# Encoder layer: places of the first W_up tiles in the sample's output projection, and the number of leading steps in the prompt's

## The chip, the cores and the metric

The kernel runs on one core of one Trainium2 chip. The metric is the device time of one execution in microseconds (us). Of several executions the median counts. Five engines work side by side, each on its own queue in order: TensorE (PE, matrix products; its weight loads are PEld), VectorE (DVE), ScalarE (ACT), GpSimd (POOL) and SyncE (SP), which here starts most of the DMA transfers. The order in each queue is fixed when the program is built; at run time an engine waits at the head of its queue until what the instruction needs is there.

## The reference

One layer of a bidirectional encoder, applied with the same weights to two request groups: `sample` (512 tokens) and `prompt` (1024 tokens), with a model width of 1024 and a hidden width of 4096. What matters here is the second half of the layer:

```python
    mixed = jax.nn.sigmoid(gate_na) * y_na + jax.nn.sigmoid(gate_fn) * y_fn
    x = x + mixed @ w_out
    a = jax.nn.relu(rmsnorm(x, g_mlp) @ w_up)
    return x + (a * a) @ w_down
```

`w_out` is 1024 x 1024, `w_up` 1024 x 4096. All is in fp32. The kernel makes an fp32 product from three products of two parts each: a number is split into a rounded part `hi` and the rest `lo`, and hi\*hi, hi\*lo and lo\*hi are added up in PSUM (`mm3`, line 122).

## The kernel before, in words

**Order of the whole.** The sample is done first (attention, Fourier mixing, gates, output projection, W_up), then the prompt, and at the end W_down for both. The program is written in one order, and a scheduler that fixes each engine's queue when the program is built takes from it, by its own model of times, what it holds to be ready, earlier lines first. So products of different tiles can stand mixed on PE. `behind(marks)` keeps instructions after given ones, and `pinned()` after the last ones written so far.

**A weight tile** (`weights`, line 142) is fetched by DMA to one of two raw places `w_raw` (512 KB), its `hi` is made by ACT (line 152) and its `lo` by POOL (line 153; one W_out tile has it on DVE). Only when POOL is done is the raw place free for the next fetch.

**The sample's output projection** (`Layer.project_out`, line 1079). W_out is cut into eight tiles, numbers 0 to 3 for the left half of the output columns, 4 to 7 for the right. Their places (line 460): number 0 in the pool `mlp` (tag `w`, two places), 1 to 4 in the pool `out` (tag `wo`, four places), 5 in two Fourier tiles, 6 in the shared `w_hi`/`w_lo` places, 7 in the second `w` place. First come the left halves of the four token tiles t = 0 to 3 (128 tokens each), then their right halves. After each right half the tile is added to x (DVE, line 1105), stored, and normed: ACT squares and sums (line 174), DVE does nine short steps on one column (lines 175 to 183) and a wide one (line 184). The normed tile is then transposed on PE (line 194) and split by ACT and DVE (lines 133 and 134) into `h2T`, the input of W_up.

**W_up of the sample** (`Up`, line 1123). 32 tiles f of 128 hidden columns; `load(f)` fetches and splits one, into the shared `w_hi`/`w_lo` places for f % 4 of 0 or 1, else into the two `w` places. `load(0)` is called after the third right half, 1 and 2 after the fourth, the others when `up(f)` begins, though the scheduler moves them ahead as soon as places are free. Tiles 0, 1 and 2 are multiplied in two halves of 256 tokens: their first halves need only token tiles 0 and 1, and the transposes of tiles 2 and 3 stand between them. The other tiles take 512 tokens at once. `run` then walks over pairs of tiles; beside each pair it does a step of `combine` (sums of W_down blocks on POOL) and a step of `reading` (norm and transposes of the prompt's first tiles).

**The prompt's output projection** (`Halves.project_out`, line 1274). Eight token tiles with a left and a right half each: 16 steps n = 0 to 15 of 24 matmuls. The list `steps` gives their order: the first four left halves, then right and left in turn, then the last four right halves (n = 12 to 15). The banks for even n are of the tag `mm`, for odd n of `o`. The k-th right half (k = 0 to 7) is normed as above. For odd k four differences of the tiles k and k-1 are formed on DVE (line 1342). An even k makes two turns, an odd k five: a turn (`turn`, line 1263) is four transposes into a PSUM bank (four banks, tags `t` and `s`) and two splits on ACT and DVE. `due` says after which step's product the turns stand: two steps after the right half (one after for n = 14, so k = 5 and k = 6 both have theirs after the last product, and k = 7 after the first products of W_up). Turns into `t2` and `t3` need the places of W_out's left half and wait until the step `freed`, one after the last left half. `ahead` splits the first W_up pair on ACT and POOL beside it. W_out's right half (tiles 4 to 7) goes to the places `w` and `r` of the pool `mlp`. After the last product come the turns of k = 5 and 6, the first W_up products with `b11` and `b21` (lines 1358 and 1361), the turns of k = 7 and the W_up product with `t2`.

Of the kernel before, what the change touches and what calls it, by code (L numbers as in the profile page):

```python
# [68 lines left out]
class Layer:  # L69
# [279 lines left out]
    def run(self, order):  # L349
# [4 lines left out]
        hp, close_hT = self.open("hT_0", "left")  # L354
        hT, folded = self.new_hT(hp, order[0][1], NM)
        for i, (name, T) in enumerate(order):
# [5 lines left out]
            if i == 0:  # L362
                with pool("first", "right") as p:
# [8 lines left out]
                    marks = self.mark((mybir.EngineType.SP,))  # L372
                    w0 = self.qk_weights(0)

                    rest = self.tables(marks)
# [20 lines left out]
            if small:  # L396
                ap, hp_, mp = (right.enter_context(pool(f"{n}_{name}", "right")) for n in ("acc", "hid", "mlp"))
# [8 lines left out]
            else:  # L406
                fn = None
                p = right_fn.enter_context(pool(f"na_{name}", "right"))
# [34 lines left out]
            with pool(f"u_{name}", "right") as up:  # L443
# [5 lines left out]
                with pool(f"dft_{name}", "right") as p:  # L449
                    fT, marks = self.fourier_positions(p, fp, name, T, u, cos, sin if small else sin + [  # L450
                        self.sines(p.tile([128, 5 * 522], F32R, name="sin"), name, T, 1)])
# [6 lines left out]
            if small:  # L458
                po = out.enter_context(pool(f"out_{name}", "right"))
# [3 lines left out]
            else:  # L463
                hp_ = right.enter_context(pool(f"hid_{name}", "right"))
# [3 lines left out]
            h2T = self.merge_fn(br, hp_ if small else br, T, fT, mixed, sig, gate, wout, marks)  # L468
            close_br()
            close_fT()  # L470
            if not small:
                mp = right.enter_context(pool(f"mlp_{name}", "right"))
                places += [(mp, [128, 2, 512], "w", 2)] * 2 + [(mp, [128, 2, 512], "r", 2)] * 2
                with self.behind(self.mark()):
                    rest = list(wout)
# [3 lines left out]
            acc = [ap.tile([128, D], F32, name=f"acc{t}") for t in range(T // 128)]  # L479
            self.short = mlp = self.Up(self, ap, hp_, mp, name, T, h2T)  # L480
            marks = self.mark()
            with self.behind(marks):
                rest = list(wout)
            self.project_out(hp_, mp, self.ins[f"x_{name}"], T, h2T, rest, acc, mlp, marks)
            out.close()
            right_fn.close()
            reading, before_last = iter(()), lambda qs: None
            if nxt:
                hp, close_hT = self.open(f"hT_{i + 1}", "left")
# [586 lines left out]

            yield self.weights(src, place and (place() if callable(place) else self.pair(*place)), lo_engine=self.nc.vector if i == 2 else None)

    def project_out(self, hp, p, x, T, m, wo, acc, mlp, marks):

        nc = self.nc
        wo = self.wo + wo
        nt = T // 128
        gain = self.gain(p.tile([128, D], F32, name="gain", bufs=1), "g_mlp")
        for t in range(nt):
            nc.sync.dma_start(acc[t], x[t * 128:(t + 1) * 128, :])
        pending = []

        def product(ps, half, t, blocks, more=False):
            ts = slice(t * 128, (t + 1) * 128)  # L1090
            w = wo[4 * half:4 * half + 4]
            self.mm3(ps, [(m[kt // 2][0][:, kt % 2, ts], m[kt // 2][1][:, kt % 2, ts], w[kt // 2][0][:, kt % 2], w[kt // 2][1][:, kt % 2])
                          for kt in blocks], more=more)
            return ps


        banks = {(0, t): product(self.psum(), 0, t, range(6)) for t in range(2)}
        for half in range(2):
            cs = slice(half * 512, (half + 1) * 512)
            for t in range(nt):  # L1100
                if (half, t) in banks:
                    ps = product(banks[half, t], half, t, range(6, 8), True)
                else:
                    ps = product(self.psum(), half, t, range(8))
                nc.vector.tensor_tensor(out=acc[t][:, cs], in0=acc[t][:, cs], in1=ps, op=ALU.add)
                if half:
                    nc.sync.dma_start(mlp.sums[t], acc[t])
                    if len(pending) == 2:
                        self.transpose_in(*pending.pop(0))
                    hn = hp.tile([128, D], F32, name="hn", bufs=2)  # L1110
                    self.norm(acc[t], gain, hn, junk=p.tile([128, 512], F32, name="relu", bufs=2).bitcast(BF16))
                    pending.append((hn, m, t * 128))
                    if t == nt - 2:
                        with self.behind(marks):
                            mlp.load(0)
        mlp.load(1)
        mlp.load(2)
        for f in range(3):
            next(mlp.ups[f])
            if pending:  # L1120
                self.transpose_in(*pending.pop(0))

    class Up:

# [8 lines left out]
            self.sums = [layer.dram.tile([128, D], F32, name=f"sum_{name}{t}") for t in range(T // 128)]  # L1133
            self.ups = [self.up(f) for f in range(self.NF)]

        def load(self, f):
            if f not in self.w:
                to = None

                if f % 4 > 1 or f >= self.NF - 4:  # L1140
                    to = [x.rearrange("p a (k c) -> p (a k) c", c=128) for x in self.layer.pair(self.p, [128, 2, 512], "w", 2)]
                self.w[f] = self.layer.weights(self.layer.rows("w_up", f * 128), to)

        def up(self, f):

            nc, T, h2T = self.nc, self.T, self.h2T
            self.load(f)
            w = self.w.pop(f)
            g, odd = divmod(f, 2)
            if g not in self.r:  # L1150
                self.r[g] = [t.bitcast(F32) for t in self.layer.pair(self.hp, [128, T], "hid", 4)]
            r = self.r[g][odd]
            step = 256 if f < 3 else 512
            for c in range(T // step):
                cs = slice(c * step, (c + 1) * step)
                ps = self.layer.psum()[:, :step]
                self.layer.mm3(ps, [(w[0][:, kt], w[1][:, kt], *(t[:, kt % 2, cs] for t in h2T[kt // 2])) for kt in range(8)])
                nc.scalar.activation(out=r[:, cs], in_=ps, func=AF.Relu)
                nc.vector.tensor_tensor(out=r[:, cs], in0=r[:, cs], in1=r[:, cs], op=ALU.mult)
                yield  # L1160
            two = lambda x: x.rearrange("p (a b) -> p a b", b=T // 2)
            to = self.hid[g // 2][:, :, g % 2]
            nc.sync.dma_start(to[:, 2 * odd:2 * odd + 2], two(r))
            if odd:
                (a11, a21), (a12, a22) = ([two(x)[:, i] for i in range(2)] for x in self.r.pop(g))
                sums = two(self.hp.tile([128, D], F32, name="hn", bufs=2))
                s1, s2, s3, s4 = (sums[:, i] for i in range(4))
                for k, x, y, op in ((s1, a21, a22, ALU.add), (s2, s1, a11, ALU.subtract), (s3, a11, a21, ALU.subtract),
                                    (s4, a12, s2, ALU.subtract)):
                    nc.vector.tensor_tensor(out=k, in0=x, in1=y, op=op)  # L1170
                nc.sync.dma_start(to[:, 4:8], sums)
# [46 lines left out]
class Halves:  # L1218
# [55 lines left out]
    def project_out(self, hp, mp, m, wo):  # L1274

        layer, nc, nt, TH = self.layer, self.nc, self.nt, self.TH
# [31 lines left out]


        order = [t // 2 + nt // 2 * (t % 2) for t in range(nt)]  # L1310
        steps = [(t, 0) for t in order[:nt // 2]]
        for k in range(nt // 2):
            steps += [(order[k], 1), (order[k + nt // 2], 0)]
        steps += [(t, 1) for t in order[nt // 2:]]
        freed = max(n for n, x in enumerate(steps) if not x[1]) + 1
        hn, ahead = [], self.ahead()
        b["t4"] = [[layer.wtile(k, [128, 2, TH]) for k in ("hi", "lo")] for _ in range(2)]
# [2 lines left out]
        for n, (t, half) in enumerate(steps):  # L1320
# [6 lines left out]
            if half:  # L1327
                k = len(hn)
# [470 lines left out]
```

## Time and profile before

| what | value |
|---|---|
| median of 3 runs | 1949.89 us |
| lowest and highest | 1944.79 and 1950.25 us |
| the profiled execution's own time | 1946.61 us |
| its span, first to last instruction | 1944.8 us |
| busy DVE, ACT, POOL | 1150.8, 733.5, 813.8 us |
| mean granted clock of TensorE | 0.994 |

In the profile, the time of the sample's output projection and first W_up tiles is 294 to 369 us of the span, that of the prompt's output projection 1055 to 1170 us. A row of the timeline gives the start, the duration, the engine, the line, the operation with output and inputs, and in square brackets how long the engine had been idle and whose result it waited for; consecutive instructions of one kind are merged (x4), and then the duration runs from the first start to the last end. Matmuls overlap in the pipeline: a row of one lasts 0.39 us, though the next begins 0.23 us later. A row of the windows gives the stretch, its length, the busy time of PE, PEld, DVE, ACT and POOL with their instruction counts, the granted clock (1.00 is full), the busy share of the DMA engines and GB/s.

### The profile page before, as it was taken

What the parts mean: (1) busy time and instruction counts of PE and PEld (TensorE: products, weight loads), DVE (VectorE), ACT (ScalarE), POOL (GpSimd) and SP (SyncE); (2) the same over time, 40 slices, a digit from 0 to 9 for tenths busy, and PEclk for the clock granted to TensorE, in tenths of its full rate; (3) what the DMA queues carried; (4) which work ended last, traced back from release to release, by engine and by line L of the source; (5) the groups of instructions that cost most, each with busy time, mean ns of one, the idle gap of its engine ahead of it and who ended that gap; (6) DMA issues with size and microseconds to landing.
All of it is one profiled execution on the core that took longest, in us unless ns stands there. A gap on an engine that the chain in (4) does not pass through costs nothing.

```text
span 1944.8 us, 26239 instructions
## 1 busy us (share of the span) xinstructions
PE 1898.2 (98%) x9435; PEld 1592.6 (82%) x9435; DVE 1150.8 (59%) x1917; ACT 733.5 (38%) x1292; POOL 813.8 (42%) x672
## 2 busy tenths in 40 slices
PE   7999999999999999999999999999999999999997
PEld 5888888888888888888898878888887888888885
DVE  6771755898625566550436576665665326758668
ACT  3664332443215566532223143333333323323333
POOL 1344653555512233342234218888872323323331
PEclk9999999999999999999999999999999999999999
DMA  6756953787756455463443333445446858558733
GB/s 219 202 145 225 278 180 121 223 265 247 240 174 174 132 133 153 145 229 74 140 133 108 141 98 128 172 155 174 161 174 232 306 192 314 200 198 306 254 106 122
DMA packets 312946, 358.39 MB, mean 184 GB/s; under 512 B 51768, under 2 KB 222392, under 8 KB 312264
## 3 DMA queue, kind: packets, MB, share of 16 engines
q1 hardware_dynamic: 295056, 334.93, 52.4%
q0 software_dynamic: 17760, 21.80, 4.9%
q8 instruction: 74, 1.21, 0.3%
q14 instruction: 56, 0.46, 0.1%
HBM read 263.06 MB, written 96.16 MB: 185 GB/s over the span
## 4 chain that ended last, share of the span: by engine, by line
PE 80%; DVE 8%; DMA 5%; issue 3%; ACT 3%; POOL 2%; SPq 1%; ACTq 0%; DVEq 0%; POOLq 0%
PE ps_mm L129 21%; PE ps_o L129 19%; PE ps_s L129 16%; PE ps_t L129 10%; PE ps_mm L529 3%; PE ps_mm L530 2%; PE ps_mm L531 2%; PE ps_o L678 2%; PE ps_t L658 1%; DVE st L182 1%; POOL w_lo L153 1%; DVE h_lo L153 1%; DMA w_raw<-in_w_up 1%; DMA w_raw<-in_w_out 1%; DMA r<-in_x_prompt 1%
## 5 line engine op out<-in xcount | busy, mean ns | idle before, releaser
L153 POOL TENSOR_TENSOR w_lo<-w_raw,w_hi 128x1024 fp32r<-128x1024 f32 x71 | 177.1, 2494 | 228.0 <-ACT w_hi L152 182.2
L153 POOL TENSOR_TENSOR w_lo<-raw,w_hi 128x1024 fp32r<-128x1024 f32 (+1 forms) x49 | 101.3, 2070 | 211.6 <-ACT w_hi L152 205.7
L152 ACT CAST w_hi<-w_raw 128x1024 fp32r<-128x1024 f32 x88 | 92.4, 1050 | 177.2 <-PE ps_s L129 49.8
L153 DVE TENSOR_TENSOR h_lo<-long,h_hi 128x1024 fp32r<-128x1024 f32 x54 | 84.6, 1568 | 79.2 <-ACT h_hi L152 78.0
L529 PE MATMUL ps_mm<-hT,w_hi 128*128 128x512 f32 (+2 forms) x296 | 121.8, 411 | 0.0
L530 PE MATMUL ps_mm<-hT,w_hi 128*128 128x512 f32 (+2 forms) x296 | 110.8, 374 | 0.0
L531 PE MATMUL ps_mm<-hT,w_lo 128*128 128x512 f32 (+2 forms) x296 | 110.7, 374 | 0.0
L152 ACT CAST h_hi<-long 128x1024 fp32r<-128x1024 f32 x54 | 56.7, 1049 | 106.5 <-PE ps_s L129 30.0
L153 DVE TENSOR_TENSOR hs_lo<-short,hs_hi 128x512 fp32r<-128x512 f32 x54 | 63.1, 1168 | 42.5 <-ACT hs_hi L152 42.5
L652 ACT ACTIVATE sc<-sc,ast 128x288 f32<-128x288 f32 (+4 forms) x96 | 53.9, 561 | 72.4 <-DVE ast L650 72.0
L1392 POOL TENSOR_TENSOR x<-w_hi,x 128x512 fp32r<-128x512 f32 (+1 forms) x42 | 70.9, 1687 | 16.3 <-ACT x L1395 16.3
L152 ACT CAST w_hi<-raw 128x1024 fp32r<-128x1024 f32 (+1 forms) x49 | 40.9, 839 | 88.5 <-DVE raw L1608 51.9
L678 PEld LDWEIGHTS ps_o<-pt,vb 104*64 104x64 f32 (+6 forms) x576 | 62.8, 164 | 10.7 <-POOL vb L615 2.6
L678 PE MATMUL ps_o<-pt,vb 104*64 104x128 f32 (+6 forms) x576 | 62.6, 245 | 2.8 <-POOL vb L615 1.2
L531 PEld LDWEIGHTS ps_mm<-hT,w_lo 128*128 128x128 f32 x296 | 55.9, 189 | 10.3
L129 PE MATMUL ps_t<-gate,x 128*128 128x512 f32 x264 | 63.7, 391 | 0.0
L615 POOL TENSOR_TENSOR vb<-vr,vb 96x384 fp32r<-96x384 f32 (+4 forms) x48 | 48.5, 1029 | 34.6 <-ACT vb L614 33.8
L129 PE MATMUL ps_mm<-gate,x 128*128 128x512 f32 x256 | 62.6, 390 | 0.0
L650 DVE CUSTOM_DVE_ANT_0 sc<-ps_s,bm 128x288 f32<-128x288 f32 (+4 forms) x96 | 46.3, 482 | 24.8 <-issue 10.5
L772 POOL MEMSET bm<- 64x96 f32 (+2 forms) x64 | 11.2, 175 | 118.2 <-DVE ast L650 92.5
L129 PEld LDWEIGHTS ps_t<-gate,x 128*128 128x128 f32 x264 | 49.4, 188 | 11.0 <-DVE r_lo L1505 0.8
L530 PEld LDWEIGHTS ps_mm<-hT,w_hi 128*128 128x128 f32 x296 | 56.5, 191 | 1.6
(687 smaller groups left out, 5595.7 us busy)
## 6 DMA issues: line engine op xcount, KB each, us to landing
long<-hidden_prompt SPq DMA_DIRECT2D x54, 512.0 KB
w_raw<-in_w_in SPq DMA_DIRECT2D x52, 512.0 KB
raw<-in_w_down SPq DMA_DIRECT2D x39, 512.0 KB
w_raw<-in_w_up SPq DMA_DIRECT2D x34, 512.0 KB
hidden_prompt<-h SPq DMA_DIRECT2D x32, 512.0 KB
short<-hidden_sample SPq DMA_DIRECT2D x54, 256.0 KB
w_lo<-in_w_down SPq DMA_DIRECT2D x18, 512.0 KB
w_raw<-in_w_out SPq DMA_DIRECT2D x16, 512.0 KB
```

What stands on the lines that cost most here:

```text
L129: self.nc.tensor.matmul(out, a, b, start=(i == 0 and not more), stop=(i == len(terms) - 1), skip_group_check=more)
L152: nc.scalar.copy(out=hi, in_=raw)
L153: (lo_engine or nc.gpsimd).tensor_tensor(out=lo, in0=raw, in1=hi.bitcast(F32), op=ALU.subtract)
L182: nc.vector.scalar_tensor_tensor(out=a, in0=y, scalar=y, in1=v, op0=ALU.mult, op1=ALU.mult)
L529: nc.tensor.matmul(ps, a[0], b[0], start=(kt == 0), stop=False)
L530: nc.tensor.matmul(ps, a[0], b[1], start=False, stop=False)
L531: nc.tensor.matmul(ps, a[1], b[0], start=False, stop=(kt == 7))
L615: nc.gpsimd.tensor_tensor(out=lo, in0=vs, in1=hi.bitcast(F32), op=ALU.subtract)
L650: nc.vector.tensor_tensor_reduce(out=sc[:, :W], in0=ps[:, :W], in1=bm[:, :W], scale=1.0, scalar=3e38, op0=ALU.add, op1=ALU.min, accum_out= ...
L652: nc.scalar.activation(out=sc[:, :W], in_=sc[:, :W], func=AF.Exp, bias=st[:, 0:1], scale=-1.0, accum_out=st[:, 1:2])
L678: nc.tensor.matmul(po[:m, j * 128:(j + 1) * 128], v, x, start=(i == 0), stop=(i == len(ops) - 1))
L1392: self.nc.gpsimd.tensor_tensor(out=to, in0=x, in1=y, op=op)
```

## The change

In the sample, `load(0)` to `load(2)` are called after the right halves of t = 0, 1 and 2 with places of their own: the tag `wo`, whose tiles 1, 2 and 3 of W_out are read for the last time by the left halves. `load(3)` is called after the fourth right half and goes to a `w` place as before. Four tiles instead of three are multiplied in two halves; all four first halves stand before the second halves, and the second halves are now written in `project_out`, so that the first two rounds of `run` have nothing left to multiply and do only their steps of `combine` and `reading`. The pool `out` is closed only after that, as it is in the text of `run`.

In the prompt, `lead` is 3 instead of 4: three left halves, then right and left in turn five times, then the last three right halves (n = 13 to 15). So right half k stands at n = 3, 5, 7, 9, 11, 13, 14, 15 instead of 4, 6, 8, 10, 12, 13, 14, 15, and `freed` is 13 instead of 12.

```diff
-    def project_out(self, hp, p, x, T, m, wo, acc, mlp, marks):
+    def project_out(self, hp, p, po, x, T, m, wo, acc, mlp, marks):
...
                     pending.append((hn, m, t * 128))
-                    if t == nt - 2:
+                    if t < 3:
                         with self.behind(marks):
-                            mlp.load(0)
-        mlp.load(1)
-        mlp.load(2)
-        for f in range(3):
+                            mlp.load(t, self.pair(po, [128, 2, 512], "wo", 4))
+                    else:
+                        mlp.load(t)
+        for f in range(4):
             next(mlp.ups[f])
             if pending:
                 self.transpose_in(*pending.pop(0))
+        for f in range(4):
+            for _ in mlp.ups[f]:
+                pass
...
-        def load(self, f):
+        def load(self, f, to=None):
             if f not in self.w:
-                to = None
-
-                if f % 4 > 1 or f >= self.NF - 4:
-                    to = [x.rearrange("p a (k c) -> p (a k) c", c=128) for x in self.layer.pair(self.p, [128, 2, 512], "w", 2)]
+                if to is None and (f % 4 > 1 or f >= self.NF - 4):
+                    to = self.layer.pair(self.p, [128, 2, 512], "w", 2)
+                if to:
+                    to = [x.rearrange("p a (k c) -> p (a k) c", c=128) for x in to]
                 self.w[f] = self.layer.weights(self.layer.rows("w_up", f * 128), to)
...
-            step = 256 if f < 3 else 512
+            step = 256 if f < 4 else 512
...
-        steps = [(t, 0) for t in order[:nt // 2]]
-        for k in range(nt // 2):
-            steps += [(order[k], 1), (order[k + nt // 2], 0)]
-        steps += [(t, 1) for t in order[nt // 2:]]
+        lead = nt // 2 - 1
+        steps = [(t, 0) for t in order[:lead]]
+        for k in range(nt - lead):
+            steps += [(order[k], 1), (order[k + lead], 0)]
+        steps += [(t, 1) for t in order[nt - lead:]]
```

More of the change, by code (lines that the diff above doesn't have):

```diff
@@ L483, in run @@
                 rest = list(wout)
-            self.project_out(hp_, mp, self.ins[f"x_{name}"], T, h2T, rest, acc, mlp, marks)
+            self.project_out(hp_, mp, po, self.ins[f"x_{name}"], T, h2T, rest, acc, mlp, marks)
             out.close()
```

## The prediction

> **What bounds the kernel now.** I read the page first, then the list of PE's waits, then the windows of the two stages that the diff touches, and last the timelines around the gaps found there.
>
> ```profile
> span 1944.8 us, 26239 instructions
> PE 1898.2 (98%) x9435; PEld 1592.6 (82%) x9435; DVE 1150.8 (59%) x1917; ACT 733.5 (38%) x1292; POOL 813.8 (42%) x672
> ...
> PE ps_s L1269 <- DVE gate L134: 3.6, 1, 3.6
> ...
> PE ps_mm L129 <- ACT w_hi L152: 2.3, 1, 2.3
> ...
> PE ps_s L129 <- DVE gate L134: 2.0, 2, 1.8
> ...
> PE ps_mm L129 <- ACT r_hi L1373: 0.7, 1, 0.7
> ...
> 1055.20:1149.86 94.66, 94.51 (x450) 78.59 (x450) 53.96 (x126) 26.89 (x56) 22.37 (x12) 1.00 0.34 120
> 1149.86:1168.80 18.94, 14.04 (x73) 11.76 (x72) 15.22 (x42) 9.37 (x26) 1.27 (x1) 0.82 0.36 107
> ...
> 1156.00:1158.00 2.00, 2.00 (x12) 1.99 (x10) 0.95 (x4) 0.85 (x3) 1.27 (x1) 0.50 0.32 94
> ```
>
> PE is busy 98% of the span, and the diff takes no product away. A gain can only come out of gaps of PE and of stretches at a lowered clock. Two waits on the list lie in the changed stages: 2.0 us behind the sample's output projection and 3.6 us behind the prompt's. The windows show more: the prompt's projection keeps PE full to 1149.86 (94.51 of 94.66 us), and in the 18.94 us after that PE is busy for 14.04 only, at a mean clock of 0.82, and at 0.50 in the slice from 1156.
>
> **The end of the prompt's projection.** PE first, then DVE:
>
> ```profile
> 1151.16 0.60 PE L1269 MATMUL ps_t<-ident,h 128*128 128x128 f32 x4
> 1155.38 1.09 PE L1269 MATMUL ps_s<-ident,h 128*128 128x128 f32 x4 [3.61 <-DVE gate L134]
> ...
> 1157.82 3.63 PE L129 MATMUL ps_mm<-gate,y 128*128 128x512 f32 x8
> ...
> 1165.92 0.60 PE L1269 MATMUL ps_t<-ident,x 128*128 128x128 f32 x4
> 1166.35 0.60 PE L1269 MATMUL ps_s<-ident,h 128*128 128x128 f32 x4
> ...
> 1169.14 0.44 PE L129 MATMUL ps_s<-hid_hi,y 128*128 128x512 f32 x1
> ...
> 1141.28 0.15 DVE L175 TENSOR_SCALAR st<-st 128x1 f32<-128x1 f32 x1 [1.27 <-ACT x L174]
> ...
> 1143.19 1.28 DVE L184 SCALAR_TENSOR_TENSOR x<-x,st,gain 128x1024 f32<-128x1024 f32 x1
> ...
> 1144.99 0.69 DVE L1342 TENSOR_TENSOR h<-x,x 128x512 f32<-128x512 f32 x1
> 1145.59 0.69 DVE L1342 TENSOR_TENSOR h<-x 128x512 f32<-128x512 f32 x1
> ...
> 1149.33 0.14 DVE L175 TENSOR_SCALAR st<-st 128x1 f32<-128x1 f32 x1
> ...
> 1152.00 1.28 DVE L184 SCALAR_TENSOR_TENSOR x<-x,st,gain 128x1024 f32<-128x1024 f32 x1
> 1153.20 0.42 DVE L134 TENSOR_TENSOR gate<-ps_s,gate 128x256 fp32r<-128x256 f32 x1
> 1153.53 0.42 DVE L134 TENSOR_TENSOR gate<-ps_t,gate 128x256 fp32r<-128x256 f32 x1
> ...
> 1159.61 0.41 DVE L134 TENSOR_TENSOR gate<-ps_s,gate 128x256 fp32r<-128x256 f32 x1
> ```
>
> After the last product four turns fill the four banks (to 1151.76); the fifth waits 3.61 us, because DVE is still at the norm of k = 6 (from 1149.33 to 1153.2) and splits no bank before. Then the clock is down, and a turn takes 1.09 us merged instead of 0.60. The W_up product with t2 begins at 1169.14. From 1149.86 on PE needed 12 turns at 0.43 (1165.92 to 1166.35), 5.2 us, and 24 matmuls of 0.23, 5.4 us: 10.6 of 19.3 us. So **8.7 us** are to be had here at the most.
>
> What the change moves: the right half of k = 4 goes from n = 12 to 11, so its norm and its two turns leave the crowded end. Four held-back turns into t2 and t3 go the other way, from n = 12 to 13, because `freed` is one later. DVE's account for the time from the end of n = 13 to the end of n = 15: a norm takes 3.1 us (1141.28 to 1144.4), the four differences 2.4 (0.6 from start to start), a turn 0.66 (two splits at 0.33 from start to start, 1153.20 to 1153.53), an addition 0.6. After the change: two additions 1.2, six turns 4.0, the norm and differences of k = 5, 5.5, the norm of k = 6, 3.1, together **13.8 us**, with some 13.5 us of PE there (two products of 5.4 and six turns of 0.43). I count from 1136: turns of 0.43 that stand before that product are three more than now, those behind it fewer. So the norm of k = 6 ends near 1151.2, 2.0 us before its 1153.2 of now; the one POOL subtraction that can hold a difference up (next part) is in both. What was late next is the splits: seven turns, 14 x 0.33 = 4.6 us from 1151.2, to 1156 instead of 1159.6. PE's gap shrinks from 3.6 to about 1.6 us. At that length I expect the clock to hold, since a gap of 1.76 us in the sample left it at 1.00 (next part) and this one of 3.61 did not. Then: product with b11 ends near 1157.6, copy of the bank 0.7 (the wait on L1373), product with b21 to 1161, where 1165.92 stands now; DVE has the norm and differences of k = 7 at 1161.5 (1156 and 5.5); the t2 product begins 3.2 us after PE's first turn, as now (1165.92 to 1169.14), near 1164.5. **I take -4.5 us**; the bounds are 0 (the gap stays) and -8.7.
>
> [...]
>
> **The beginning of the prompt's projection.**
>
> ```profile
> 1071.56 0.39 PE L129 MATMUL ps_o<-hid_hi,gate 128*128 128x512 f32 x1
> ...
> 1079.72 0.39 PE L129 MATMUL ps_mm<-r_hi,gate 128*128 128x512 f32 x1
> ...
> 1075.97 1.05 ACT L152 CAST r_hi<-w_raw 128x1024 fp32r<-128x1024 f32 x1 [5.31 <-DMA w_raw<-in_w_out]
> ...
> 1077.11 2.39 POOL L153 TENSOR_TENSOR r_lo<-w_raw,r_hi 128x1024 fp32r<-128x1024 f32 x1 [3.95 <-ACT r_hi L152]
> ```
>
> Now the first right half is n = 4 and meets W_out's tile 7 at its 13th matmul, 1079.72, just after POOL has done it (1079.50). With three leading steps the first right half is n = 3 and begins at 1071.56; its 13th matmul would come at 1074.3, **5.2 us too early**. The cover: n = 4 is a left half whose weights are all there, it takes 5.4 us, and its bank is free. If the scheduler puts it into the hole, the cost is 0. It must have foreseen the hole, though, by a model of DMA, ACT and POOL; where it expects tile 7 too early, PE waits in order for the difference. The nearest rows are the longest wait of PE for a weight tile in the list above, 2.3 us, and no wait; the bounds are 0 and 5.2. **I take +1.5**, between the two. Added beside it: no instruction; queues keep their order of loads.
>
> **The sample.**
>
> ```profile
> 360.15 2.88 PE ps_mm L129 x24
> 363.04 5.47 PE ps_s L129 x24
> ...
> 340.90 0.39 PE L129 MATMUL ps_s<-gate,w_hi 128*128 128x256 f32 x1
> ...
> 346.97 0.63 PE L129 MATMUL ps_s<-gate,w_hi 128*128 128x256 f32 x3 [1.76 <-DVE gate L134]
> ...
> 339.52 1.06 ACT L152 CAST w_hi<-w_raw 128x1024 fp32r<-128x1024 f32 x1 [1.26 <-PE ps_mm L129]
> ...
> 344.20 2.36 POOL L153 TENSOR_TENSOR w_lo<-w_raw,w_hi 128x1024 fp32r<-128x1024 f32 x1 [1.16 <-ACT w_hi L152]
> ...
> 344.23 2.34 DVE L182 SCALAR_TENSOR_TENSOR st<-st 128x1 f32<-128x1 f32 x1
> ...
> 346.50 0.41 DVE L134 TENSOR_TENSOR gate<-ps_t,gate 128x256 fp32r<-128x256 f32 x1
> ```
>
> From 340.9 PE has six half products of 2.88, one whole of 5.47 and two transposed tiles (some 0.8 each): 24.4 us, done by 365.3; it is done at 368.5. So 3.2 us are lost. 1.76 of them have this cause: a one-column step of the fourth norm takes 2.34 us, just as long as POOL works on a `lo`, and behind it in DVE's queue stands the last split of token tile 1 (346.50), on which PE waits. That POOL work is tile f = 3. The rest, 1.4 us, are short gaps while tile 1 comes in, with f = 1 only cast at 339.52, since its place was read by the last W_out product.
>
> Added: tile 3 as two halves costs 2 x 2.88 - 5.47 = +0.3. Saved: tiles 0 to 3 are ready before 340, so up to three quarters of four half products (8.6 us of work) lie beside the gaps; I take -1.0 of the 1.4. The 1.76, I think, mostly stay: the raw places run on, tile 5 takes the very place that f = 1 waited for, and tile 6 the `w` place of f = 3, so two POOL pieces of 2.4 us fall where two fall now, and PE, in order, waits at tile 0's last quarter however much other work stands behind. I take -0.3 of it, a small chance of its going. The four POOL pieces brought ahead (320 to 330) meet norms 0 and 1, whose transposes have 4 us to spare. **Sum -1.0 us**, bounds +0.3 and -2.9. The later close of the pool `out` holds the prompt's input tile back only until about 366, and that is first written after 380; I cost it at 0.
>
> [...]
>
> **The sum.** -4.5 + 1.5 - 1.0 = **-4.0 us** against the profiled execution's 1946.6 us (span 1944.8 and 1.8 around it): 1942.6. The median shown is 1949.9, 3.3 us above that execution; from there it would be 1945.9. I predict between the two, **1944.2 us**. 0.3%, about what a measurement of this kernel can tell from no change, is 5.8 us, so the forecast is a gain too small to be told.
>
> **The rivals.**
>
> *Most of both losses goes.* The scheduler puts the splits of k = 5 before the norm of k = 7 with no gap, the fill at the projection's start works, and POOL misses the fourth norm: -6.5, 0 and -2 us, **-8.5**, 1938 on the profiled scale. For it: both losses hang on single instructions of DVE's queue. Against it: 13.8 us of DVE work for 13.5 of PE.
>
> *The wait moves to W_out.* Place: the 13th matmul of n = 3. If the left half n = 4 isn't put there, PE waits 5.2 us; that is above the 3.61 us that brought the clock to 0.50, so some 5.6 us (1155.4 to 1161) run at half speed, another 2.8. +8.0 - 4.5 - 1.0 = **+2.5**: slower than before, at 1949.1 to 1952.4. It decides where wait and clock together cost 5.5 us, which uses the gains up. For it: tile 7 has 0.2 us to spare now and is wanted 5.4 us earlier. Against it: PE's queue mixes products elsewhere.
>
> [...]
>
> **How the numbers follow.** Forecast (-2 to -5.8) 0.42, most of both 0.30, no effect 0.15, the wait at W_out 0.13. The range goes from the second case on the profiled scale, 1938, to the third on the median's, 1951. Faster by over 0.3%: the second case and the forecast's edge, 0.33. Slower by over 0.3%: the W_out wait with no gain at the end, 0.09. Within: 0.58.
>
> **What would show it.** At the end of the prompt's projection: PE's longest gap under 2 us, the granted clock at 1.00, 14 to 15 us from the last product to the t2 product instead of 19.3. At its start: matmuls of n = 4 between the 12th and 13th of n = 3, any wait there for `r_lo` or `r_hi`. In the sample: whether a POOL `lo` stands beside the fourth norm, and PE's wait of 1.8 us with it. I am wrong if DVE's order at n = 13 puts the held-back turns so that the norm of k = 6 ends no earlier, or if the scheduler's new order costs PE somewhere that the diff doesn't touch.

## The result, and the profile after

| | before | after |
|---|---|---|
| median of 6 runs each on one chip, us | 1948.1 (1944.8 to 1950.3) | 1960.2 (1954.0 to 1965.5) |
| ratio after to before | | 1.0062, 95% interval 1.0042 to 1.0082 |
| span of the profiled execution, us | 1944.8 | 1957.6 |

The change makes the kernel 12 us slower (8 to 16 by the interval); 1944.2 us was forecast, a gain. In what follows a ratio is turned into microseconds with 1948 us.

The page of the kernel after, and its list of PE's waits (the line, what it waited for, microseconds in total, times, longest):

```profile
span 1957.6 us, 26286 instructions
PE 1902.3 (97%) x9459; PEld 1595.5 (82%) x9459; DVE 1147.6 (59%) x1918; ACT 733.4 (37%) x1293; POOL 814.6 (42%) x672
...
PE ps_s L129 <- DVE gate L134: 4.8, 2, 4.7
PE ps_s L1272 <- DVE gate L134: 3.0, 1, 3.0
...
PE ps_o L129 <- ACT r_hi L152: 2.5, 1, 2.5
...
PE ps_o L129 <- POOL r_lo L153: 1.6, 1, 1.6
```

PE's work is the same but for the 24 more rows of the split fourth tile; the busy time of 1902.3 instead of 1898.2 us is for the most part matmuls at a lowered clock: PE is busy for 19.1 us of the slices at 0.50, before for 12.6, and by my estimate half of the difference, 3.3 us, is the clock's. Of the two waits that the change aimed at, the sample's has grown from 1.8 to 4.7 us and the prompt's has shrunk from 3.6 to 3.0. Two new ones stand at the beginning of the prompt's output projection.

In what follows a cast is ScalarE's half of a split (L152), a GpSimd difference or piece the other half (L153), the Square ScalarE's part of a norm (L174), and a slice a stretch of 3.41 us, for one or more of which the granted clock falls to 0.50 (last section).

To see where the time goes, I followed each matmul from one trace into the other and noted how much later it comes (one execution each, us):

```
stretch                                            later at its start   at its end   share
start to the sample's output projection                    0               +1.5      +1.5
sample: end of W_out to the end of f = 3                 +1.5              +9.2      +7.7
sample's other W_up tiles, prompt's attention            +9.2              +8.4      -0.9
prompt's output projection and its end                   +8.4             +14.9      +6.5
prompt's W_up and W_down                                +14.9             +13.2      -1.8
```

The first and the last row are code that the change doesn't touch: a slice at half clock falls in the one execution and not in the other (from 160.2 us after, from 1488.8 us before). **Two stretches make the loss, some 7 us each**, and both are places that the change edits.

**The sample.** ScalarE's rows of the kernel before, around its first norm, and VectorE's addition that makes the norm's input:

```profile
324.00 1.05 ACT L152 CAST w_hi<-w_raw 128x1024 fp32r<-128x1024 f32 x1 [6.29 <-DMA w_raw<-in_w_up]
324.96 1.06 ACT L174 ACTIVATE relu<-acc 128x1024 bf16<-128x1024 f32 x1
...
322.55 0.69 DVE L1105 TENSOR_TENSOR acc<-acc,ps_mm 128x512 f32<-128x512 f32 x1 [4.81 <-PE ps_mm L129]
```

The same place after, in the timeline of ScalarE, then of GpSimd, VectorE and PE:

```profile
325.80 1.05 ACT L152 CAST wo_hi<-w_raw 128x1024 fp32r<-128x1024 f32 x1 [3.71 <-DMA w_raw<-in_w_up]
329.49 1.05 ACT L152 CAST w_hi<-w_raw 128x1024 fp32r<-128x1024 f32 x1 [2.64 <-DMA w_raw<-in_w_up]
330.45 1.05 ACT L174 ACTIVATE relu<-acc 128x1024 bf16<-128x1024 f32 x1
...
344.77 2.35 POOL L153 TENSOR_TENSOR w_lo<-w_raw,w_hi 128x1024 fp32r<-128x1024 f32 x1 [7.08 <-ACT w_hi L152]
347.08 1.26 POOL L1190 TENSOR_TENSOR acc<-acc,acc 128x512 f32<-128x512 f32 x1
...
324.07 0.69 DVE L1105 TENSOR_TENSOR acc<-acc,ps_mm 128x512 f32<-128x512 f32 x1 [4.80 <-PE ps_mm L129]
...
344.82 2.32 DVE L183 SCALAR_TENSOR_TENSOR st<-st 128x1 f32<-128x1 f32 x1
347.17 2.25 DVE L184 SCALAR_TENSOR_TENSOR hn<-acc,st,gain 128x1024 f32<-128x1024 f32 x1
349.95 0.41 DVE L134 TENSOR_TENSOR gate<-ps_t,gate 128x256 fp32r<-128x256 f32 x1
...
350.41 1.01 PE L129 MATMUL ps_s<-gate,wo_hi 128*128 128x256 f32 x3 [4.66 <-DVE gate L134]
```

Two things are to be seen. The Square of the first norm (L174) starts 5.5 us later. 1.5 of them the kernel brought along; what it reads is there at 324.8 (the end of the addition), so it waits 5.7 us, where it waited 1.7 before (323.2 to 324.96, behind one cast: the trace of before had the same wait in small). Four casts of W_up tiles now stand ahead of it in ScalarE's queue, and the last two of them wait 3.71 and 2.64 us for their DMAs. And the third norm is held up twice on VectorE: a step of 0.16 us lasts 2.32 beside a GpSimd difference of a later W_up tile (344.77), and the wide multiply of 1.28 us lasts 2.25 beside GpSimd's first sum for W_down (347.08). That sum is `pinned()` behind the instructions written ahead of it, and those are done early now (it ran at 373 us before). The split at 349.95, on which PE waits 4.66 us, stands behind both. Two slices at half clock (347.9 to 354.8) are part of the 7.7 us.

**The beginning of the prompt's projection.** PE, then ScalarE, GpSimd and VectorE:

```profile
1079.94 0.39 PE L129 MATMUL ps_o<-w_hi,gate 128*128 128x512 f32 x1
...
1085.30 0.79 PE L129 MATMUL ps_o<-r_hi,gate 128*128 128x512 f32 x1 [2.47 <-ACT r_hi L152]
1087.72 0.79 PE L129 MATMUL ps_o<-r_lo,gate 128*128 128x512 f32 x1 [1.63 <-POOL r_lo L153]
...
1092.34 0.39 PE L129 MATMUL ps_mm<-hid_hi,gate 128*128 128x512 f32 x1
...
1084.20 1.04 ACT L152 CAST r_hi<-w_raw 128x1024 fp32r<-128x1024 f32 x1 [4.93 <-DMA w_raw<-in_w_out]
...
1085.33 2.34 POOL L153 TENSOR_TENSOR r_lo<-w_raw,r_hi 128x1024 fp32r<-128x1024 f32 x1 [3.58 <-ACT r_hi L152]
...
1079.51 0.69 DVE L1310 TENSOR_TENSOR x<-x,ps_mm 128x512 f32<-128x512 f32 x1 [10.80 <-DMA x<-in_x_prompt]
```

The first right half, n = 3, begins at 1079.94 and meets tile 7 at its 13th matmul, as forecast; it would come at 1082.67, the cast ends 2.6 us later, and the difference, 1087.67, 4.8 us behind the 14th. No matmul of n = 4 stands in the hole; its first is the row of 1092.34, behind all of n = 3. Its bank was not what kept it out: VectorE adds the first bank to x at 1079.51, late because x comes by DMA, but the bank is free at 1080.2, 2.5 us ahead of the hole. The matmuls behind the wait take 0.79 instead of 0.39 us, at a granted clock of 0.50. Without a hole n = 4 would have begun near 1085.4. So 6.9 us are lost, 4.1 of them in the two waits and 2.8 by the clock.

**The end of the prompt's projection.** The windows of the projection and of the stretch to the W_up product with t2 (columns as in the prediction), then the timeline:

```profile
1063.58:1166.20 102.62, 97.60 (x449) 80.14 (x449) 56.84 (x128) 26.79 (x56) 22.27 (x12) 0.97 0.30 108
1166.20:1184.07 17.87, 13.56 (x75) 10.94 (x73) 14.87 (x41) 9.60 (x27) 1.27 (x1) 0.90 0.42 129
```

```profile
1163.69 1.82 DVE L1346 TENSOR_TENSOR h<-x,h 128x512 f32<-128x512 f32 x1
...
1167.14 1.28 DVE L184 SCALAR_TENSOR_TENSOR x<-x,st,gain 128x1024 f32<-128x1024 f32 x1
1168.35 0.68 DVE L1310 TENSOR_TENSOR x<-x,ps_o 128x512 f32<-128x512 f32 x1
...
1163.67 1.29 POOL L1396 TENSOR_TENSOR y<-w_raw,y 128x512 fp32r<-128x512 f32 x1 [15.69 <-ACT y L1399]
...
1169.11 1.06 ACT L174 ACTIVATE x<-x 128x1024 f32<-128x1024 f32 x1 [1.02 <-DVE x L1310]
...
1171.12 1.09 PE L1272 MATMUL ps_s<-ident,h 128*128 128x128 f32 x4 [3.01 <-DVE gate L134]
```

The norm of k = 6 ends at 1168.35, 2.15 us behind the last product; before it was 3.34 (1153.2 against 1149.86). From the last product to the t2 product it takes 17.87 us instead of 19.28. PE's gap is 3.01 us, not the 1.6 forecast: the second copies of the two banks that PE waits for stand behind the Square of k = 7 on ScalarE (1169.11 to 1170.16), and that Square waits for the last addition, which VectorE does only behind the norm of k = 6 (1168.35).

### The profile page after: what moved, and what is told of

Read it like the earlier page. It is cut to its first block, busy times and chain, and to the rows that moved or that the text cites. A ratio compares the mean times of both kernels' runs of the same rounds, so it can differ in the third digit from the quotient of the medians.

```text
span 1957.6 us, 26286 instructions
## 1 busy us (share of the span) xinstructions
PE 1902.3 (97%) x9459; PEld 1595.5 (82%) x9459; DVE 1147.6 (59%) x1918; ACT 733.4 (37%) x1293; POOL 814.6 (42%) x672
## 4 chain that ended last, share of the span: by engine, by line
PE 79%; DVE 7%; issue 5%; DMA 4%; POOL 3%; ACT 2%; SPq 0%; ACTq 0%; DVEq 0%; POOLq 0%
PE ps_mm L129 20%; PE ps_o L129 19%; PE ps_s L129 16%; PE ps_t L129 10%; PE ps_mm L529 3%; PE ps_mm L530 3%; PE ps_mm L531 2%; PE ps_o L678 2%; POOL w_lo L153 1%; PE ps_t L658 1%; DMA w_raw<-in_w_out 1%; DVE st L182 1%; DVE h_lo L153 1%; DVE st L183 1%; PE ps_t L194 1%
## 5 line engine op out<-in xcount | busy, mean ns | idle before, releaser
L153 POOL TENSOR_TENSOR w_lo<-w_raw,w_hi 128x1024 fp32r<-128x1024 f32 x68 | 173.4, 2550 | 228.6 <-ACT w_hi L152 185.4
L153 POOL TENSOR_TENSOR w_lo<-raw,w_hi 128x1024 fp32r<-128x1024 f32 (+1 forms) x49 | 101.2, 2069 | 209.8 <-ACT w_hi L152 203.5
L152 ACT CAST w_hi<-w_raw 128x1024 fp32r<-128x1024 f32 x85 | 89.3, 1051 | 160.4 <-PE ps_o L129 48.2
L153 DVE TENSOR_TENSOR h_lo<-long,h_hi 128x1024 fp32r<-128x1024 f32 x54 | 84.6, 1567 | 79.3 <-ACT h_hi L152 72.9
L152 ACT CAST h_hi<-long 128x1024 fp32r<-128x1024 f32 x54 | 56.7, 1050 | 108.5 <-issue 34.9
L153 DVE TENSOR_TENSOR hs_lo<-short,hs_hi 128x512 fp32r<-128x512 f32 x54 | 61.1, 1132 | 40.3 <-ACT hs_hi L152 39.3
L152 ACT CAST w_hi<-raw 128x1024 fp32r<-128x1024 f32 (+1 forms) x49 | 40.9, 839 | 88.7 <-DVE raw L1612 51.5
L129 PEld LDWEIGHTS ps_t<-gate,x 128*128 128x128 f32 x264 | 49.4, 188 | 10.9 <-DVE r_lo L1509 0.8
```

Of the source, the lines that this page charges most:

```text
L129: self.nc.tensor.matmul(out, a, b, start=(i == 0 and not more), stop=(i == len(terms) - 1), skip_group_check=more)
L152: nc.scalar.copy(out=hi, in_=raw)
L153: (lo_engine or nc.gpsimd).tensor_tensor(out=lo, in0=raw, in1=hi.bitcast(F32), op=ALU.subtract)
```

## The experiments

Ten kernels, each timed against the kernel before in five rounds on the same chip. "Stage" is the share of the stretch in one execution, counted as in the table above.

**1 and 2: each part of the change alone.** The prompt's part is the edit of `steps`, with everything else as before; the sample's part is the rest.

```diff
         order = [t // 2 + nt // 2 * (t % 2) for t in range(nt)]
-        steps = [(t, 0) for t in order[:nt // 2]]
...
+        lead = nt // 2 - 1
+        steps = [(t, 0) for t in order[:lead]]
...
```

> The prompt's three leading first halves alone, the sample as before. Theory (the change's two parts each cost some 7 us of their own): +5 to +8 us against before, made of a wait of 2.5 us for the seventh W_out tile's cast, 1.6 us for its difference and a half-speed window of some 7 us behind them, with the end of the projection gaining 0 to 1 us. Rival (the sample's part costs all of it, and the prompt's waits only follow from being late there): within 2 us of before.

> The sample's part alone, the prompt with four leading first halves as before. Theory: +6 to +8 us against before, with the first norm's Square standing behind four casts on ScalarE (about 330.5 instead of 325.0 us of the span). Rival (the prompt's part costs all): within 2 us of before.

The prompt's part alone: ratio 1.0026 (1.0015 to 1.0037), +5.1 us. The sample's part alone: 1.0041 (1.0027 to 1.0056), +8.0 us. Their sum, 13.1, agrees with the change's 12 (8 to 16). The prompt's kernel waits 2.9 and 1.6 us for tile 7, and the sample's shows its Square behind the casts again, 6 us after its data. So the two losses add up, and each is made where it is seen.

**3, 4 and 5: the sample's two causes.** The edit of run 3, against the sample's part alone:

```diff
                     pending.append((hn, m, t * 128))
-                    if t < 3:
-                        with self.behind(marks):
-                            mlp.load(t, self.pair(po, [128, 2, 512], "wo", 4))
-                    else:
-                        mlp.load(t)
+                    if t == 0:
+                        square = self.mark((mybir.EngineType.Activation,))
+                    with self.behind(marks + square if t > 1 else marks):
+                        mlp.load(t, self.pair(po, [128, 2, 512], "wo", 4) if t < 3 else None)
```

> The sample's part alone, with the casts of W_up's tiles 2 and 3 queued behind the first norm's Square on ScalarE. Theory A (the Square that stands behind the casts makes the loss): the Square comes back to about 325 us, all four norms 4 to 5.5 us earlier, PE's wait of 4.7 us goes and its half-speed window with it; total -1 to +2 us against before. Theory B (GpSimd's pieces brought forward, the W_up splits and the W_down sum, hold the norms on VectorE wherever they fall): the Square is early but the norm steps still take 2.3 us beside GpSimd's pieces; total +4 to +8 us against before.

Ratio 1.0010 (1.0001 to 1.0019), +2.0 us. Its timeline of ScalarE, GpSimd, VectorE and PE:

```profile
323.52 1.06 ACT L174 ACTIVATE relu<-acc 128x1024 bf16<-128x1024 f32 x1 [2.84 <-DVE acc L1105]
...
325.74 2.39 POOL L153 TENSOR_TENSOR wo_lo<-w_raw,wo_hi 128x1024 fp32r<-128x1024 f32 x1 [2.59 <-ACT wo_hi L152]
...
333.40 2.38 POOL L153 TENSOR_TENSOR w_lo<-w_raw,w_hi 128x1024 fp32r<-128x1024 f32 x1 [0.92 <-ACT w_hi L152]
341.63 2.35 POOL L153 TENSOR_TENSOR w_lo<-w_raw,w_hi 128x1024 fp32r<-128x1024 f32 x1 [5.85 <-ACT w_hi L152]
...
325.72 2.42 DVE L182 SCALAR_TENSOR_TENSOR st<-st 128x1 f32<-128x1 f32 x1
...
333.39 2.42 DVE L182 SCALAR_TENSOR_TENSOR st<-st 128x1 f32<-128x1 f32 x1
...
341.68 2.32 DVE L183 SCALAR_TENSOR_TENSOR st<-st 128x1 f32<-128x1 f32 x1
...
346.31 1.01 PE L129 MATMUL ps_s<-gate,wo_hi 128*128 128x256 f32 x3 [3.69 <-DVE gate L134]
```

Neither theory was whole. The Square is back at 323.5 and most of the loss goes, as A says; but each of the four norms now has one step of 2.3 to 2.4 us beside a GpSimd piece (the fourth at 348.7), as B says, and PE still waits 3.69 us. The pieces at 333.40 and 341.63 belong to the next W_up tiles, f = 4 and 5 (that of 325.74 to f = 2): since tiles 0 to 2 no longer take the usual places, those tiles find them free and are cast while the norms run. Runs 4 and 5 hold their casts back until the last copy of the fourth token tile's transposes:

```diff
             if pending:
                 self.transpose_in(*pending.pop(0))
+                mlp.hold = self.mark((mybir.EngineType.Activation,))
...
-            self.load(f)
+            with self.layer.behind(self.hold):
+                self.load(f)
             w = self.w.pop(f)
```

Run 4 has this in the sample's part as the change has it, run 5 together with the edit of run 3.

> The sample's part with the tiles from 4 on cast late, but the first Square behind the casts as in the change. If the two causes add up (the Square 6 us, the held steps 2 to 4 us), the Square stays at about 330 us and the time is +3 to +6 us against before. If the held steps make nearly all of it, within 2 us of before. If the Square makes nearly all of it, +7 to +9 us as the sample's part alone.

> The run with casts 2 and 3 behind the first Square, and W_up's tiles from 4 on cast only behind the last copy of the fourth token tile's transposes. Theory AB (two causes in the sample: the Square behind the casts, worth some 6 us by the runs so far, and the GpSimd differences of tiles 4 to 6, which their free places now let run beside norms 1 to 3, each stretching one step to 2.3 us): norm 1, 2 and 3 each keep all their steps under 0.3 us, unless GpSimd's sum for W_down comes in; PE's wait of 3.7 us falls under 1.5; total -3 to 0.5 us against before. Rival (the rest is only the clock's slices of half speed that fall by chance): the steps run freely, but the time stays within 1 us of the run with the ordered casts, +1 to +3 us against before.

Run 4: 1.0010 (1.0001 to 1.0018), +1.9 us, its Square still at 329.9, with its data there at 323.95; PE's wait is 1.8 us. That is below the +3 to +6 us expected if both causes count, and inside "within 2 us of before", the range of the held steps alone; but run 3, which keeps the held steps and has the Square early, is at +2.0 too. Run 5: 0.9985 (0.9976 to 0.9994), **-2.9 us**. The Squares of runs 4 and 5, and the sample's line in run 5's list of PE's waits, where the wait is gone:

```profile
329.92 1.05 ACT L174 ACTIVATE relu<-acc 128x1024 bf16<-128x1024 f32 x1
...
324.30 1.06 ACT L174 ACTIVATE relu<-acc 128x1024 bf16<-128x1024 f32 x1 [2.88 <-DVE acc L1105]
...
PE ps_s L129 <- DVE gate L134: 0.2, 1, 0.2
```

The first norm of run 5 still has a step of 2.24 us beside the piece of f = 2, and PE doesn't wait for it: this held step costs nothing.

| sample's part | total against before | stage, one execution |
|---|---|---|
| as changed | +8.0 (5.3 to 10.9) | +8.2 |
| Square ahead of casts 2 and 3 | +2.0 (0.2 to 3.7) | +4.9 |
| tiles from 4 on late | +1.9 (0.2 to 3.5) | +3.9 |
| both | -2.9 (-4.7 to -1.2) | -1.4 |

From the last row upward, the late Square alone costs 4.8 us, the held steps alone 4.9, and both 10.9; by the intervals of the runs, each difference is sure to some 2.4 us, and that of both to some 3.3. The single effects were expected unequal (6 and 2 to 4); within that they are alike. The +4.9 of run 3's execution holds a slice at half clock that falls right behind its gap of 3.69 us.

**6: GpSimd's sums for W_down.** Run 5's kernel with its first steps of the sums held back by two pairs of tiles.

```diff
-                with layer.pinned():
-                    next(combining, None)
+                for _ in range((0, 0, 2, 2)[g] if g < 4 else 1):
+                    with layer.pinned():
+                        next(combining, None)
```

> As the run with the late tiles, and GpSimd's first W_down sums held back by two pairs of tiles. Theory: they cost the fourth norm up to one held step; 0 to 2 us faster than the run with the late tiles, -4 to 0 us against before. Rival: nothing of them stands beside a norm any more, and the time is that of the run with the late tiles within 0.7 us.

Ratio 0.9997 (0.9988 to 1.0006): -0.6 us, 2.3 us more than run 5. Both theories missed. The stage gains 0.6 us more (-2.0), but PE now waits for norms of the prompt's tokens, which are normed beside the sample's W_up:

```profile
PE ps_t L194 <- DVE r L184: 3.8, 2, 2.9
...
425.40 2.39 POOL L153 TENSOR_TENSOR w_lo<-w_raw,w_hi 128x1024 fp32r<-128x1024 f32 x1 [0.59 <-ACT w_hi L152]
...
425.37 2.43 DVE L182 SCALAR_TENSOR_TENSOR st<-st 128x1 f32<-128x1 f32 x1
```

What holds the step here is a difference of a W_up tile, not a sum. In run 5 the same norm has a held step too (2.25 us), but its Square starts at 419.88 instead of 422.18, and PE waits 0.51 us for it. The two sums now run at 419.8 to 422.4 instead of 414.6 to 417.6, and the differences behind them in GpSimd's queue come later with them; that this is what makes the norm late is likely and not shown.

**7 and 8: the late tile 7 of the prompt.** Run 7 keeps the end of the change and the beginning of before: four left halves, then two right halves, and the fourth left half moved behind the first right half.

```diff
         steps += [(t, 1) for t in order[nt - lead:]]
+        steps[lead:lead + 3] = [steps[lead + i] for i in (1, 0, 2)]
```

> The prompt's part alone, but with a fourth first half ahead of the first second half, and the fourth moved back only behind that (four first halves, two second halves, then by turns): the end of the projection is that of the change, its beginning that of before. Theory A (the loss is the seventh W_out tile, wanted 5.4 us earlier than it is ready): no wait and no half speed at the beginning; total -3 to +1 us against before, by what the end gains. Theory B (any shorter lead costs VectorE its norms' time, two second halves in a row most of all): waits on the bank or the norm in the middle of the projection, +3 us or more against before.

Ratio 0.9992 (0.9983 to 1.0000): -1.6 us. There is no wait for W_out, and two right halves in a row cost nothing that shows. The interval reaches 1, so the gain over before is at its edge; that the loss of 5.1 us is gone is clear. So what the change loses there, it loses to the tile. Run 8 leaves the order of the change and makes the low parts of W_out's tiles 3 to 7 on VectorE (`small` is true for the sample alone):

```diff
-            yield self.weights(src, place and (place() if callable(place) else self.pair(*place)), lo_engine=self.nc.vector if i == 2 else None)
+            yield self.weights(src, place and (place() if callable(place) else self.pair(*place)), lo_engine=self.nc.vector if i == 2 or i > 2 and not small else None)
```

> The prompt's part alone, with the low parts of W_out's tiles 3 to 7 made on VectorE, which has nothing to do there, instead of GpSimd: 1.3 us each instead of 2.4, so the places for the raw tiles come free sooner and tile 7 should be ready some 2.5 us earlier. If the late tile is the cause of the loss, PE waits 1 to 2 us instead of 4.1 there, with or without a slice at half speed; total +0 to +3 us against before, 2 us or more under the prompt's part alone. If the loads are held up by the x tiles beside them rather than by the raw places, tile 7 comes no earlier and the time stays at +4 to +6 us.

Ratio 1.0000 (0.9991 to 1.0010), 5.1 us under the prompt's part alone. The difference of tile 7 and PE's only wait there:

```profile
1076.76 1.22 DVE L153 TENSOR_TENSOR r_lo<-w_raw,r_hi 128x1024 fp32r<-128x1024 f32 x1 [1.50 <-ACT r_hi L152]
...
1078.04 0.50 PE L129 MATMUL ps_o<-r_lo,gate 128*128 128x512 f32 x1 [0.56 <-DVE r_lo L153]
```

The raw places come free sooner, since the difference takes 1.22 us on VectorE where GpSimd took 2.34 in the kernel after: the fetch of tile 7 is issued at 1070.24 us instead of 1072.43 in run 1. The wait of 2.9 + 1.6 us is down to 0.56, better than expected.

**9 and 10: both mends, and the end.** Run 9 is the whole change with the edits of runs 5 and 7.

> The whole change with both mends: the sample's tiles from 4 on cast late and its casts 2 and 3 behind the first Square; four first halves ahead in the prompt, the fourth moved back behind that. If the parts are independent, the sum of the two runs that mended one part each: -2.9 and -1.6 us against their own runs of before (taken over their intervals' middles), -4.5 us, between -7 and -2; 10 us or more under the change as made. If the gains were the clock's chance, within 1.5 us of before.

Ratio **0.9969 (0.9957 to 0.9981), -6.0 us** (-8.4 to -3.7), median 1941.5 us: faster than before and 18 us under the change. The parts add up, within the interval. Run 10 also moves GpSimd's piece (1163.67 above) behind the last product:

```diff
-            if n >= len(steps) // 2 - 1:
+            if len(steps) // 2 - 1 <= n < len(steps) - 2:
```

> As the run with both mends, and the combining of W_up's weights that is handed out beside the prompt's last two products comes only behind them, so that GpSimd's piece of 1.3 us stands beside no norm or difference at the end of the projection. If VectorE held up by that piece (1.82 instead of 0.68 us) is what keeps the norm of k = 6 late, that norm ends 1.1 us earlier, PE's gap of 3.0 us falls to some 1.9, and the time is 0.5 to 2 us under the run with both mends. If the gap hangs on the splits' order instead, or W_up's pieces come late for the next products: no gain, or 1 to 3 us slower.

Ratio 0.9972 (0.9963 to 0.9982), -5.5 us: no gain over run 9 that these runs could tell. PE's timeline:

```profile
1154.85 0.63 PE L1273 MATMUL ps_s<-ident,h 128*128 128x128 f32 x4 [1.91 <-DVE gate L134]
...
1195.43 3.01 PE L129 MATMUL ps_t<-gate,x 128*128 128x512 f32 x12 [1.02 <-DVE r_lo L1511]
```

The step is right: the held difference falls from 1.82 to 0.69 us, and PE's gap from 3.01 to 1.91, by the 1.1 expected. The gain is given back 40 us later: a wait of 1.02 us that run 9's trace doesn't have at that place, and 0.4 us in small gaps.

## Why the prediction was wrong

**The sample: -1.0 forecast, +7.7 in the trace, +8.0 by run 2.** The step that failed is "The four POOL pieces brought ahead (320 to 330) meet norms 0 and 1, whose transposes have 4 us to spare". It counted GpSimd's half of a split and not ScalarE's: each piece has a cast before it, and the last cast waits for a DMA at the head of a queue in which the first norm's Square is next. The second step that failed is "two POOL pieces of 2.4 us fall where two fall now": the reading looked at the places of tiles 5 and 6, and not at the usual places which tiles 0 and 1 no longer take, so that tiles 4 and 5 move up as well; W_down's sums move up too. Run 5 shows that a gain was there: with both causes away, which takes more edits than the change has, the stage is 1.4 us shorter in the trace (forecast -1.0), and the whole by 2.9 (1.2 to 4.7).

**The beginning of the prompt's projection: +1.5 forecast, +7 in the trace, +5.1 for the whole part by run 1.** The hole was found, its time (5.2 us) and its tile were right, and the rival named it with its price of 8.0. What failed is the choice "between the two", +1.5: n = 4 didn't go into the hole, "PE waits in order for the difference", and the clock fell on top (4.1 and 2.8 us). Nothing in the trace of before showed PE's queue mixing left and right halves there. "Its bank is free" held when the hole came. Why the scheduler left n = 4 behind n = 3 stays open; run 7, which writes a left half ahead of the right one by hand, has neither the wait nor the loss.

**The end: -4.5 forecast.** The trace of after gives -1.4 from the last product on (19.28 to 17.87) and takes 1.0 of it back ahead of that (the projection's 7.96 us more, less the 7.0 at its beginning), -0.4 together. 0.8 of that 1.0 is a wait of PE for a difference on VectorE, at 1140.87 us, which the kernel before doesn't have and for which the forecast has no term. The account of VectorE had the norm of k = 6 end 2.0 us nearer to the last product; it is 1.2 nearer. The gap is 1.4 us longer than forecast: 0.8 is this norm, held by GpSimd's piece (1.82 instead of 0.68 us; run 10, without it, has a gap of 1.91). The other 0.6 is the last addition, which now stands between this norm and the Square of k = 7, and so ahead of the second copies behind that Square: again ScalarE's queue, which the forecast left out. Where the clock holds (runs 7 and 9, gaps of 3.04 and 3.01 us) the projection and its end together are worth -1.6 us in the traces, and part of that is the clock's penalty of before. So the mechanism was there, and the term was mis-sized by 3 us.

**The clock.** "At that length I expect the clock to hold, since a gap of 1.76 us in the sample left it at 1.00 (next part) and this one of 3.61 did not" reads the clock by the length of a gap. The last section shows that the length alone doesn't decide: the gap of 3.01 us of the kernel after cost a slice at half clock (from 1170.5), that of 3.04 in run 7 none. The case without effect (0.15, and the range's upper end of 1951 us) was reckoned with a length above which a gap costs the clock. No run shows such a length: half clock came behind the gap of 2.47 us of the kernel after, and the clock stayed at 1.00 behind that of 3.04.

**The sum.** The rival "the wait moves to W_out" (0.13) was the nearest; it gave +2.5 because it took the end at -4.5 and the sample at -1.0. No rival had the sample on the other side, and that is what put the time outside the range. What was asked of the trace was which engine is late for PE; for the edit that brings work forward, the question that was missing is what stands behind it on ScalarE.

## What to carry to other kernels

Work that is brought forward into free places stands ahead of something in each queue that it uses, and a load that ends in a cast can put a DMA wait at the head of ScalarE's queue (here 3.71 and 2.64 us); with the casts of tiles 2 and 3 held behind the first Square and the later ones behind the norms' last copies, the same edit turned from +8 to -3 us. Freed places are taken by the next in line, too, so follow the whole chain of loads and not only those that the diff names. Where a reordering wants a tile earlier, ask the trace for that tile's last two steps, and write the work that is to fill the hole ahead by hand, as run 7 does, before counting on the scheduler to put it there.

## What the runs showed of the hardware

**In these traces the clock changes by fixed slices of 3.413 us.** All changes of the granted clock in one execution lie a whole number of such slices apart, here for the kernel after (starts of its stretches at half clock, us of the span; the last one, 524 slices from the first, runs into the program's end):

```
start     160.2   347.9   798.5   1085.2   1170.5
slices        0    55.0   187.0    271.0    296.0
length     3.41    6.83    3.41     6.83     3.41
```

Half clock follows slices in which PE's busy share is low (counted below). The windows of three kernels, one slice a row (behind the length stands PE's busy time, and behind those of the five engines the granted clock); first the kernel after:

```profile
1081.86:1085.27 3.41, 0.97 (x5) 0.50 (x3) 0.00 (x0) 1.04 (x1) 0.00 (x0) 0.99 1.00 398
1085.27:1088.69 3.42, 1.76 (x3) 1.11 (x4) 0.65 (x1) 0.00 (x0) 2.34 (x1) 0.50 1.03 422
```

The kernel before, at the end of the projection:

```profile
1150.90:1154.31 3.41, 0.86 (x8) 0.62 (x6) 3.34 (x9) 2.06 (x4) 0.00 (x0) 1.00 1.00 313
1154.31:1157.72 3.41, 2.35 (x11) 2.38 (x12) 2.29 (x8) 2.54 (x9) 1.27 (x1) 0.50 0.64 177
```

Run 7 at the same place, and its gap there:

```profile
1155.87:1159.28 3.41, 1.55 (x15) 1.31 (x13) 3.30 (x8) 1.96 (x4) 0.00 (x0) 1.00 0.99 292
1159.28:1162.70 3.42, 2.22 (x14) 1.74 (x15) 2.94 (x11) 3.35 (x13) 1.27 (x1) 1.00 1.01 320
...
1160.46 0.63 PE L1269 MATMUL ps_s<-ident,h 128*128 128x128 f32 x4 [3.04 <-DVE gate L134]
```

The gap of 2.47 us in the kernel after lies in one slice, with PE busy for 0.97 of 3.41 us, and the next slice is at 0.50; that of 3.04 in run 7 lies across two, with 1.55 and 2.22, and the clock stays at 1.00. Over the twelve profiled executions, each cut into its own slices (without the first 16 to 18 us, for which the traces have no clock, and without the program's end), all 17 slices at full clock with PE busy for less than 0.41 of them were followed by half clock, none of some 6600 above 0.60, and 22 of the 45 between (PE's ends are modelled, so the edge is blurred). So in these runs whether a gap of 2.5 to 3.1 us cost a slice at half clock (by my estimate up to 1.7 us, half of 3.41, or more where two slices follow) hung on how it lay to the slices. Part of the scatter of a kernel's time goes with the clock: run 9's executions go from 1940.51 us at a mean granted clock of 0.997 to 1946.15 at 0.994.

**A one-column step of VectorE can last as long as a GpSimd instruction.** With 0.22 us by itself, it took 2.42 us where it began beside a GpSimd difference of 2.39 (325.72 above); the wide multiply of 1.28 took 2.25 beside the sum at 347.08; in these rows each GpSimd piece holds one VectorE instruction and then lets the next through. A split, which reads PSUM, was not held beside such a piece (in the kernel before 0.42 us at 341.32, beside a piece from 340.66 to 343.04; the same 0.42 us at 1153.20, where no piece runs).
